# One decoder layer on one core: inputs laid out by the host, a new emission order, and a new last expert group

## The chip, the cores and the metric

The kernel runs on one core of a Trainium2 chip. TensorE (PE; its weight loads are PEld), VectorE (DVE), ScalarE (ACT) and GpSimd (POOL) each run their own queue in order; SyncE (SP) issues the DMAs. The metric is the device time of one execution in microseconds. The kernel before takes 398.06 us, the median of three runs from 396.9 to 398.94.

## The reference, cut to what matters

One layer for 256 tokens of width 1024 in float32: RMSNorm, one input projection (3592 columns) that feeds eight attention heads and four gated-DeltaNet heads, an output projection, a residual add; then RMSNorm and a mixture of 32 experts in four routing groups, of which each token uses two; a residual add and a last RMSNorm.

```
h = rmsnorm(x, attn_norm)
proj = einsum('bsd,de->bse', h, w_in)           # mq mk mv | gqkv gz ga gb
y_a = moba_attention(mq, mk, mv)
gqkv = silu(causal_depthwise_conv(gqkv, conv_w))
y_b = rmsnorm(gated_delta_rule(l2norm(gq), l2norm(gk), gv, log_decay, beta), gdn_norm) * silu(gz)
x = x + einsum('bse,ed->bsd', concat([y_a, y_b]), w_out)
h = rmsnorm(x, ffn_norm)
y = sum over experts e:  combine[t, e] * (silu(h @ w_gate[e]) * (h @ w_up[e])) @ w_down[e]
return rmsnorm(x + y, final_norm)
```

## The kernel before, in words

**Two halves.** The first half is everything up to the router. Its work is cut into some 300 named steps (generators that issue a few instructions each), and the long string `ORDER` says in which order the steps go out; each engine runs its own instructions in that order. The second half takes the experts four at a time: `NG` = 8 groups (not the routing groups). Every expert has three weight slabs of 1 MB (gate, up, down), so 96 MB go through SBUF. `load_expert` (L492) issues the next slab as soon as a buffer of 2048 columns is free; there are 25 such buffers, most of which serve the first half before, and become free there one by one. All loads go through SP's one queue, in order.

**The first half.** The input projection is done as three products of split numbers: weights are split into a high part (ACT cast, L561) and a low part (a subtraction, L563, on DVE or POOL as the string `LOW` says), and x likewise (`X.h`, L461 and L463: `hH`, `hL`). A piece `P0` to `P55` (L585, for one of the groups L594) is the twelve products of one block of 128 input channels with 512 output columns; pieces of one output group add up in two of the eight PSUM banks. x comes in by rows and is turned by sixteen PE transposes (`X.tr`, L414); `X.t` copies the turned x, `X.prm` turns the convolution weights; `X.sq`, `X.rs` and `X.bc` make the inverse root mean square, which the first readers of the banks need (`conv`, L614: a product, three taps L624, a last product L630 on DVE). The output projection (`W`, L1258) does the same split with `w_out`, whose columns stand interleaved by eight: the source of its casts and subtractions is read with a stride of eight.

**A group of experts.** DVE makes a selection matrix; PE gathers the tokens (L1439), multiplies with the gate and up slabs (L1455), DVE and ACT make the hidden activations (L1673 to L1685), PE multiplies with the down slabs (`down`, L1690), ACT copies the result to SBUF (L1702) and PE adds it into four banks by the transposed selection (`spread`, L1694).

**The last group.** Its up slabs come in three pieces each (`LASTU`), its down slabs in four column blocks `LAST` of 512, 256, 128 and 128, for all four experts before the next block. `keep` puts spare products (L1637) between the up products. While these end, DVE adds what the other groups summed to x (L1733). Per block: `down`, an ACT copy (L1768), `spread`, two DVE additions and two POOL products by the last gain (`finish`, L1744 and L1745), two ACT squares with row sums (`square`, L1750). `SPR` and `SQ` set how these interleave across blocks. Then DVE finds the inverse root of each half of the tokens (`rsqrt_steps`: a first guess from the number's bits and two refinements), three engines scale the rows, and two DMAs store them (L1790).

## Time and profile before

| | |
|---|---|
| median of the runs | 398.06 us |
| the profiled execution's own time | 400.69 us |
| its span, first to last instruction | 399.0 us |
| busy: PE, DVE, ACT, POOL | 344.1, 185.3, 111.1, 80.0 us |
| granted TensorE clock, mean | 0.966 of 2.4 GHz |
| DMA | 122.4 MB, 307 GB/s over the span |

The profile page divides the span into 40 slices: PE is over 80% busy in all but the last, DVE falls from nine tenths to two tenths after the first half, and the DMA engines are at nine tenths or more from slice 18 (180 us) to slice 37. Shares of the whole span mix these two halves, so each is read by itself below.

### The profile page before, as it was taken

What the parts mean: (1) busy time and instruction counts of PE and PEld (TensorE: products, weight loads), DVE (VectorE), ACT (ScalarE), POOL (GpSimd) and SP (SyncE); (2) the same over time, 40 slices, a digit from 0 to 9 for tenths busy, and PEclk for the clock granted to TensorE, in tenths of its full rate; (3) what the DMA queues carried; (4) which work ended last, traced back from release to release, by engine and by line L of the source; (5) the groups of instructions that cost most, each with busy time, mean ns of one, the idle gap of its engine ahead of it and who ended that gap; (6) DMA issues with size and microseconds to landing.
All of it is one profiled execution on the core that took longest, in us unless ns stands there. A gap on an engine that the chain in (4) does not pass through costs nothing. (4 is left out here: it accounts for less than half of the span.)

```text
span 399.0 us, 7995 instructions
## 1 busy us (share of the span) xinstructions
PE 344.1 (86%) x3323; PEld 249.9 (63%) x3323; DVE 185.3 (46%) x467; ACT 111.1 (28%) x240; POOL 80.0 (20%) x112
## 2 busy tenths in 40 slices
PE   3999989899989997988978969788797978979990
PEld 2999989897768886888742726245272532626540
DVE  3769899987726899336420121202012120123065
ACT  3765454634434456634001000010100001000032
POOL 7138334510842218430000000000000000000033
PEclk9999999999989999999899999899998999999996
DMA  8988556725303554989999999999999999999962
GB/s 287 266 294 330 218 163 244 251 86 212 107 0 107 168 207 175 415 291 373 414 387 421 413 422 418 408 421 418 409 424 421 406 419 421 409 423 397 343 178 106
DMA packets 35353, 122.40 MB, mean 307 GB/s; under 512 B 6082, under 2 KB 9203, under 8 KB 27635
## 3 DMA queue, kind: packets, MB, share of 16 engines
q1 hardware_dynamic: 35314, 121.87, 79.3%
q8 instruction: 27, 0.44, 0.4%
q14 instruction: 12, 0.09, 0.1%
HBM read 120.81 MB, written 1.05 MB: 305 GB/s over the span
## 5 line engine op out<-in xcount | busy, mean ns | idle before, releaser
L1442 DVE TENSOR_TENSOR B<-bank,late 128x512 f32<-128x512 f32 x16 | 11.1, 691 | 83.6 <-PE bank L1439 83.6
L1745 POOL TENSOR_TENSOR K<-K,B 128x128 f32<-128x128 f32 (+2 forms) x8 | 5.6, 734 | 209.9 <-DVE K L1744 209.9
L1694 PE MATMUL bank<-B,t1k 128*128 128x512 f32 (+2 forms) x72 | 32.1, 570 | 11.3 <-ACT B L1702 11.0
L1455 PE MATMUL bank<-B,B 128*32 128x256 f32 x240 | 40.1, 381 | 0.0
L1690 PE MATMUL bank<-B,t1k 128*32 128x512 f32 (+2 forms) x104 | 37.1, 696 | 1.0 <-DVE t1k L1685 1.0
L1702 ACT COPY B<-bank 128x512 f32<-128x512 f32 x14 | 8.2, 585 | 92.6 <-PE bank L1690 92.6
L1694 PEld LDWEIGHTS bank<-B,t1k 128*128 128x128 f32 x72 | 11.8, 189 | 35.1 <-ACT B L1702 26.7
L585 PE MATMUL bank<-hL,whl 128*128 128x256 f32 x192 | 31.3, 286 | 0.0
L585 PE MATMUL bank<-hH,whl 128*128 128x256 f32 x192 | 31.1, 286 | 0.0
L1455 PE MATMUL bank<-EX,B 128*32 128x256 f32 x368 | 28.6, 380 | 0.0
L1439 PEld LDWEIGHTS bank<-t1k,B 128*128 128x128 f32 x224 | 26.0, 192 | 2.9 <-issue 2.9
L1667 DVE COPY t1k<-bank 128x256 f32<-128x256 f32 x8 | 3.4, 424 | 51.9 <-PE bank L1665 51.9
L585 PEld LDWEIGHTS bank<-hL,whl 128*128 128x128 f32 x192 | 26.3, 191 | 0.7 <-issue 0.6
L585 PEld LDWEIGHTS bank<-hH,whl 128*128 128x128 f32 x192 | 26.3, 191 | 0.2
L1439 PE MATMUL bank<-t1k,B 128*128 128x128 f32 x224 | 26.1, 275 | 0.0
L1455 PE MATMUL bank<-K,B 128*32 128x256 f32 x144 | 26.0, 380 | 0.0
L1673 ACT ACTIVATE t1k<-bank 128x256 f32<-128x256 f32 x8 | 3.1, 383 | 75.4 <-PE bank L1455 66.5
L1690 PE MATMUL bank<-EX,t1k 128*32 128x512 f32 x64 | 22.2, 675 | 1.5 <-DVE t1k L1685 1.5
L561 ACT CAST whl<-RG 128x512 fp32r<-128x512 f32 x30 | 21.2, 727 | 7.3 <-PE bank L1258 3.5
L1455 PEld LDWEIGHTS bank<-B,B 128*32 128x32 f32 x240 | 19.0, 110 | 5.2
L1455 PEld LDWEIGHTS bank<-EX,B 128*32 128x32 f32 x368 | 15.2, 110 | 6.8
L1690 PE MATMUL bank<-whl,t1k 128*32 128x512 f32 (+2 forms) x56 | 18.0, 507 | 0.6 <-DVE t1k L1685 0.5
(381 smaller groups left out, 817.1 us busy)
## 6 DMA issues: line engine op xcount, KB each, us to landing
EX<-in_w_up_dram SPq DMA_DIRECT2D x16, 1024.0 KB, 15.0
B<-in_w_gate_dram SPq DMA_DIRECT2D x12, 1024.0 KB, 19.4
B<-in_w_down_dram SPq DMA_DIRECT2D x11, 1024.0 KB, 19.9
EX<-in_w_down_dram SPq DMA_DIRECT2D x8, 1024.0 KB, 20.0
EX<-in_w_gate_dram SPq DMA_DIRECT2D x7, 1024.0 KB, 9.6
B<-in_w_in_dram SPq DMA_DIRECT2D x5, 1024.0 KB, 5.5
RG<-in_w_in_dram SPq DMA_DIRECT2D x5, 1024.0 KB, 5.1
K<-in_w_gate_dram SPq DMA_DIRECT2D x5, 1024.0 KB, 19.4
```

Of the source, the lines that this page charges most:

```text
L561: S.copy(out=hv, in_=src)
L585: PE.matmul(o_, lhsT=a_[:, c4, j * P:(j + 1) * P], rhs=b_[:, c, :], start=(c == 0 and j % 2 == 0 and n == 0), stop=(c == KC - 1 and j % 2 ...
L1439: PE.matmul(ps[:, c4 * P:(c4 + 1) * P], lhsT=x2[tt][:, q * 4 + c4, :], rhs=Dsv[:, tt], start=(tt == 0), stop=(tt == 1))
L1442: V.tensor_tensor(out=xeT[:, q * 4:q * 4 + 4, :], in0=ps.rearrange("p (c s) -> p c s", c=4), in1=ffnT[:, q * 4:q * 4 + 4].unsqueeze(2).bro ...
L1455: PE.matmul(ps[r, 0:FF], lhsT=xeT[:, c, r], rhs=w[q][0][:, c, :], start=(c == 0), stop=(c == KC - 1), tile_position=(0, q * 32))
L1667: V.tensor_copy(out=DwT, in_=pt[:, 0:T])
L1673: S.activation(out=hid, in_=pgu[0][:, 0:FF], func=AF.Tanh, scale=0.5)
L1690: PE.matmul(ps[r, 0:w], lhsT=hv[:, ft, r], rhs=wd[q][0][:, ft, c0:c0 + w], start=(ft == 0), stop=(ft == 1), tile_position=(0, q * 32))
L1694: PE.matmul(ps[tt][:, 0:w], lhsT=DwT[:, tt * P:(tt + 1) * P], rhs=ye, start=(grp == 0 or last), stop=(grp >= NG - 2), skip_group_check=True)
L1702: S.copy(out=ye, in_=ps)
L1745: G.tensor_tensor(out=xf[:, tt, cs], in0=x3s[:, tt, cs], in1=fnB[:, cs], op=ALU.mult)
```

## The change

The host now hands over the inputs in the layout that SBUF wants (`_layout`): x turned (`xt`) beside x by rows, the small parameters in one array, `w_in` and `w_out` as whole tiles with 8 KB per partition (the interleaving of `w_out` undone), the down slabs with 8 KB per partition, and the last group's up and down slabs regrouped: an up slab is two blocks of input channels for all four experts, a down slab 256 output columns for all four. The PE transposes of x and of the convolution weights, and the copies behind them, go. `LAST` becomes 256, 256, 256, 128, 128; the interleaving by `SPR` and `SQ` goes. The last inverse root becomes one POOL instruction, a power of -0.5 on two columns. `ORDER` and `LOW` are new: 14 of 72 subtractions are on POOL, 22 before.

```
-LAST = ((0, 512), (512, 256), (768, 128), (896, 128))
-LASTU = ((0, 4), (4, 2), (6, 2))
+LAST = ((0, 256), (256, 256), (512, 256), (768, 128), (896, 128))
-SPR = (3, 2, 4, 4)
-CUT = (384, 512)
+CUT = 640
 ORDER = """
-C.b*8 X.d1 X.sq C.d*5 C.a*2 C.b*2 X.d3 X.d4 X.rs X.sq*2 X.rs X.tr0 X.tr1 X.d0 X.tr0*2 X.tr1*2 X.h0 X.rs*3 X.h0 ...
+C.b*5 X.h0 X.d0 X.h2 X.d1 X.h2 X.h1 C.a X.h0 X.h3 S0 S1 S0 X.d2 X.h1 C.b X.h3 C.b*2 R.k S1 P0 C.a P0*2 S2 P1 ...
-LOW = "VVVVGVGVVVVVVVVVVVVVVVGVGVVVVGVVVGGVVVGGVGVVGVGVGGGVVVGGVVVVVGVVGVGVGVVG"
+LOW = "VVVVVVVVVVVVVVVVVVVVVVVVVVVVGVVVVVVVVVGGVGVGGGVVVVVVVGGGVVVVVGVVVGGGVVVV"
...
+    nc.sync.dma_start(out=PAR[:, 0:64], in_=par[:, 0:64])
+    for k in range(4):
+        nc.sync.dma_start(out=xT[:, 2 * k:2 * k + 2, :], in_=xt[:, 2 * k:2 * k + 2, :])
+        if k == 1:
+            load_tile(0)
     load_tile(1)
+    nc.sync.dma_start(out=PAR[:, 64:NPAR], in_=par[:, 64:NPAR])
+    nc.sync.dma_start(out=view(B0, 0, 2, D), in_=x)
...
     def xh(c):
         def go():
-            src = st["xb"][c // 2][:, (c % 2) * T:(c % 2 + 1) * T]
+            src = xT[:, c, :]
...
-                src = view(raw[j], 0, 2, D)[:, w % 2, nh * 512:(nh + 1) * 512].rearrange("p (q c) -> p c q", c=KC)
+                src = view(raw[j], 0, 2, KC, P)[:, w % 2, nh * 4:(nh + 1) * 4, :]
...
+        if grp == NG - 1 and kind:
+            for k in range(2 if kind == 2 and q == EG - 1 else 1):
+                cs = slice(k * D, (k + 1) * D) if kind == 2 and q == EG - 1 else slice(0, 2 * D)
+                nc.sync.dma_start(out=t[:, cs], in_=(w_ul, w_dl)[kind - 1][q, :, cs])
...
+    pl = {}
+    for ci, (c0, w) in enumerate(LAST):
+        ps = bank()
+        for q in range(EG):
+            down(ps, q, c0, w)
+        ye = yes[:, c0:c0 + w]
+        S.copy(out=ye, in_=ps[:, 0:w])
+        banks.give(ps)
+        pl[ci] = [bank() for _ in range(2)]
+        spread(pl[ci], w, ye)
+        finish(ci)
+        for tt in range(2):
+            square(ci, tt)
...
+    G.tensor_tensor(out=rs3, in0=ms, in1=mhalf.broadcast_to([P, 2]), op=ALU.pow)
+    S.activation(out=xf[:, 1, 0:CUT], in_=xf[:, 1, 0:CUT], func=AF.Copy, scale=rs3[:, 1:2])
+    V.tensor_scalar(out=xf[:, 0, :], in0=xf[:, 0, :], scalar1=rs3[:, 0:1], scalar2=None, op0=ALU.mult)
+    V.tensor_scalar(out=xf[:, 1, CUT:], in0=xf[:, 1, CUT:], scalar1=rs3[:, 1:2], scalar2=None, op0=ALU.mult)
...
+def _layout(np, v):
+    win, wo = v["w_in"][0], v["w_out"][0]
+    tiles = np.stack([win[:, c0:c0 + 512].reshape(P, KC, 512)[:, hh * 4:hh * 4 + 4].reshape(P, 2048) for _, c0 in GROUPS for hh in range(2)])
+    wout = wo.reshape(4, 2, P, P, KC).transpose(0, 2, 1, 4, 3).reshape(4, P, 2048)
...
```

**SP, the first loads.** Before (x by rows, then the small parameters; `RG` and `B_86` take the first two weight tiles):

```order
L208 DMA B_79<-in_x_dram 128x1024 x2
L226 DMA K_59<-in_attn_norm_dram 128x8
L228 DMA K_59<-in_conv_w_dram 48x128
L229 DMA K_59<-in_gdn_norm_dram 1x128
L219 DMA RG_88<-in_w_in_dram 128x2x512 x2
L219 DMA B_86<-in_w_in_dram 128x4x512
L234 DMA K_59<-in_w_in_dram 128x8x8
```

Now (`xt` is the turned x, `par` the small parameters):

```order
L222 DMA K_59<-in_par_dram 128x64
L224 DMA B_80<-in_xt_dram 128x512 x2
L212 DMA RG_88<-in_w_in_dram 128x1024 x2
L224 DMA B_80<-in_xt_dram 128x512 x2
L212 DMA B_86<-in_w_in_dram 128x2048
L228 DMA K_59<-in_par_dram 128x256
L229 DMA B_79<-in_x_dram 128x2048
```

The turned x and the first weight tile lead; x by rows, which the root mean square is made from, has moved from the first place to the eleventh.

**PE, from its first instruction.** Before (L260 are spare products, L414 the transposes of x, L424 that of the convolution weights; the first piece, L585, comes behind the last row):

```order
L260 MATMUL bank_67<-K_58 128x256
L260 MATMUL bank_68<-K_58 128x256
L260 MATMUL bank_69<-K_58 128x256
L414 MATMUL bank_70<-late,B_79 128x128 x4
L260 MATMUL bank_74<-K_58 128x256
L414 MATMUL bank_71<-late,B_79 128x128 x2
L414 MATMUL bank_72<-late,B_79 128x128 x2
L414 MATMUL bank_71<-late,B_79 128x128 x2
L414 MATMUL bank_72<-late,B_79 128x128 x2
L414 MATMUL bank_73<-late,B_79 128x128 x2
L424 MATMUL bank_67<-late,K_59 128x49
L414 MATMUL bank_73<-late,B_79 128x128 x2
```

Now (L252 are the spare products, L531 the pieces):

```order
L252 MATMUL bank_67<-EX_94 128x256
L252 MATMUL bank_68<-EX_94 128x256
L252 MATMUL bank_69<-EX_94 128x256
L531 MATMUL bank_70<-hH,whl_99 128x256 x2
L531 MATMUL bank_71<-hH,whl_99 128x256 x2
L531 MATMUL bank_70<-hL,whl_99 128x256 x2
L531 MATMUL bank_71<-hL,whl_99 128x256 x2
```

The first piece now follows the spare products directly.

**ACT, the last group.** Before (L1768 copies a block's `down` result, L1750 squares a finished block, L1787 scales the output):

```order
L1768 COPY B_81<-bank_69 128x512
L1768 COPY B_81<-bank_67 128x256
L1750 ACTIVATE EX_93,late<-K_60 128x512
L1768 COPY B_81<-bank_71 128x128
L1750 ACTIVATE EX_93,late<-K_60 128x512
L1750 ACTIVATE EX_93,late<-K_60 128x256
L1768 COPY B_81<-bank_74 128x128
L1750 ACTIVATE EX_93,late<-K_60 128x256
L1750 ACTIVATE EX_93,late<-K_60 128x128 x4
L1787 ACTIVATE K_58<-K_58,late 128x384 x2
```

Now (L1710 copies, L1702 squares, L1724 scales):

```order
L1710 COPY B_81<-bank_67 128x256
L1702 ACTIVATE B_80,late<-K_60 128x256 x2
L1710 COPY B_81<-bank_68 128x256
L1702 ACTIVATE B_80,late<-K_60 128x256 x2
L1710 COPY B_81<-bank_73 128x256
L1702 ACTIVATE B_80,late<-K_60 128x256 x2
L1710 COPY B_81<-bank_72 128x128
L1702 ACTIVATE B_80,late<-K_60 128x128 x2
L1710 COPY B_81<-bank_71 128x128
L1702 ACTIVATE B_80,late<-K_60 128x128 x2
L1724 ACTIVATE K_58<-K_58,late 128x640
```

Before, a copy stood ahead of the squares of the block before it. Now both squares of a block stand ahead of the next block's copy.

## Rows read from the trace of the kernel before

**Rows 1.** Timeline, PE: start us, duration us, line, out<-in, shapes, count, idle before

```profile
13.94 0.83 PE L585 MATMUL bank<-hH,whl 128*128 128x256 f32 x4
...
30.18 0.64 PE L585 MATMUL bank<-hH,mixA 128*128 128x256 f32 x4
30.66 0.64 PE L585 MATMUL bank<-hH,whl 128*128 128x256 f32 x4
```

**Rows 2.** Timeline of the first 6 us: the load of x, its first reader

```profile
0.80 0.87 SPq L208 DMA_DIRECT2D B<-in_x_dram  x2
...
4.24 1.06 ACT L401 ACTIVATE B<-B 128x1024 f32<-128x1024 f32 x1 [2.16 <-DMA B<-in_x_dram]
```

**Rows 3.** Windows: length, PE, PEld, DVE, ACT, POOL busy, PEclk, DMA share, GB/s

```profile
30.00:80.00 50.00, 47.15 (x433) 45.83 (x433) 46.59 (x92) 26.71 (x57) 24.51 (x36) 1.00 0.67 241
```

**Rows 4.** Groups by form, DVE, 10 to 185 us: count | busy us, mean ns | idle

```profile
L563 DVE TENSOR_TENSOR mixB<-B,whl 128x512 fp32r<-128x512 f32 x12 | 12.6, 1058 | 0.9 <-ACT whl L561 0.9
...
L563 DVE TENSOR_TENSOR whl<-RG,whl 128x512 fp32r<-128x512 f32 x4 | 6.1, 1546 | 7.7 <-ACT whl L561 7.7
...
L563 DVE TENSOR_TENSOR mixA<-EX,whl 128x512 fp32r<-128x512 f32 x4 | 2.8, 689 | 2.5 <-ACT whl L561 2.5
```

**Rows 5.** The same for POOL

```profile
L563 POOL TENSOR_TENSOR mixB<-B,whl 128x512 fp32r<-128x512 f32 x8 | 10.9, 1366 | 17.8 <-ACT whl L561 13.8 <-DVE t1k L624 4.0
...
L445 POOL TENSOR_SCALAR K<-K 128x2 f32<-128x2 f32 x1 | 0.4, 420 | 0.0
```

**Rows 6.** Timeline, PE: first rows of the output projection and of what follows it

```profile
153.53 0.50 PE L1258 MATMUL bank<-mixA,B 128*128 128x256 f32 x2
...
181.14 3.66 PE L1287 MATMUL bank<-B,B 128*128 128x36 f32 x32
```

**Rows 7.** Timeline, PE: two gathers, the first work of two groups of experts

```profile
313.77 3.73 PE L1439 MATMUL bank<-t1k,B 128*128 128x128 f32 x32
...
338.41 3.73 PE L1439 MATMUL bank<-t1k,B 128*128 128x128 f32 x32
```

**Rows 8.** Windows in the second half

```profile
325.00:330.00 5.00, 2.92 (x14) 0.87 (x18) 2.23 (x6) 0.00 (x0) 0.00 (x0) 0.74 1.00 413
345.00:365.00 20.00, 16.24 (x145) 7.56 (x138) 3.79 (x8) 1.55 (x3) 0.00 (x0) 1.00 1.02 414
365.00:385.00 20.00, 18.63 (x209) 11.07 (x208) 8.37 (x13) 0.97 (x2) 0.01 (x1) 1.00 0.99 336
```

**Rows 9.** Timeline of all engines, 380 to 395 us

```profile
380.19 3.98 DVE L1733 TENSOR_TENSOR K<-bank,B 128x512 f32<-128x512 f32 x4
...
380.33 0.62 PE L1690 MATMUL bank<-whl,t1k 128*32 128x512 f32 x1
...
384.97 0.11 PEld L1690 LDWEIGHTS bank<-mixB,t1k 128*32 128x32 f32 x1 [0.76 <-DMA mixB<-in_w_down_dram]
...
386.42 0.37 ACT L1768 COPY B<-bank 128x256 f32<-128x256 f32 x1 [3.46 <-PE bank L1690]
...
386.85 1.13 PE L1694 MATMUL bank<-B,t1k 128*128 128x256 f32 x4 [0.36 <-ACT B L1768]
...
387.58 0.85 DVE L1744 TENSOR_TENSOR K<-K,bank 128x256 f32<-128x256 f32 x2 [1.81 <-PE bank L1694]
...
388.08 0.41 ACT L1750 ACTIVATE EX<-K 128x256 f32<-128x256 f32 x1
...
389.03 0.99 DVE L1744 TENSOR_TENSOR K<-K,bank 128x128 f32<-128x128 f32 x4 [0.59 <-PE bank L1694]
...
390.24 0.29 ACT L1750 ACTIVATE EX<-K 128x128 f32<-128x128 f32 x1
...
390.87 0.30 DVE L1779 SCALAR_TENSOR_TENSOR late<-late 128x1 f32<-128x1 f32 x1
...
392.66 0.48 DVE L1789 TENSOR_SCALAR K<-K,late 128x512 f32<-128x512 f32 x1
...
393.43 1.50 SPq L1790 DMA_DIRECT2D out_dram<-K  x2
```

More of the change, by code (lines that the diff above doesn't have):

```diff
@@ L200, in hybrid_layer_kernel @@
     wrS = view(B4, 1760, KC, 36)
-    x0 = x[0]
     out0 = out[0]
-    win = w_in[0].rearrange("(p c) n -> p c n", c=KC)
-    for tt in range(2):
-        nc.sync.dma_start(out=xnat[tt], in_=x0[tt * P:(tt + 1) * P, :])
     raw = {}
@@ L214, in load_tile @@
         if i < 2 * len(GROUPS):
-            c0, hh = GROUPS[i // 2][1], i % 2
-            v = view(t, 0, 4, 512)
-            for k in range(2 if i == 0 else 1):
-                ks = slice(2 * k, 2 * k + 2) if i == 0 else slice(0, 4)
-                nc.sync.dma_start(out=v[:, ks, :], in_=win[:, hh * 4 + ks.start:hh * 4 + ks.stop, c0:c0 + 512])
+            n = 2 if i == 0 else 1
+            for k in range(n):
+                ks = slice(k * 2048 // n, (k + 1) * 2048 // n)
+                nc.sync.dma_start(out=t[:, ks], in_=w_in[i, :, ks])
@@ L405, in _ @@
         S.activation(out=junk[:, 1, 512:D], in_=xnat[1][:, 512:D], func=AF.Square, accum_out=ssq[:, 2:3])
-    def xtr(tt):
-        def go():
-            if tt == 0:
-                st["xb"] = [bank() for _ in range(4)]
-            xv = xnat[tt].rearrange("t (p c) -> t c p", c=KC)
-            for c in range(KC):
-                o_ = (c % 2) * T + tt * P
-                PE.transpose(out=st["xb"][c // 2][:, o_:o_ + P], in_=xv[:, c, :], identity=ident)
-                if c % 2 and c < KC - 1:
-                    yield
-        return go
-    steps["X.tr0"], steps["X.tr1"] = xtr(0), xtr(1)
-    @step("X.prm")
-    def _():
-        ps = bank()
-        PE.transpose(out=ps[:, 0:49], in_=prm, identity=ident[0:49, 0:49])
-        yield
-        S.copy(out=prT, in_=ps[:, 0:49])
-        yield
-        S.copy(out=gn_col, in_=ps[:, 48:49])
-        banks.give(ps)
     @step("X.rs")
@@ L464, in xh @@
         return go
-    def xcopy(b):
-        def go():
-            S.copy(out=xT[:, 2 * b:2 * b + 2, :], in_=st["xb"][b].rearrange("p (c t) -> p c t", c=2))
-            banks.give(st["xb"][b])
-        return go
     for c in range(KC):
         steps[f"X.h{c}"] = xh(c)
-    for b in range(4):
-        steps[f"X.t{b}"] = xcopy(b)
     for i in range(NEX):
@@ L1649, in hybrid_layer_kernel @@
             if grp or ki:
-                for i, _ in enumerate(products(pgu[ki], wx)):
+                for i, _ in enumerate(products(pgu[ki], wx, last and ki)):
                     if last and ki:
@@ L1750, in square @@
         S.activation(out=sq3[:, tt, c0:c0 + w], in_=x3s[:, tt, c0:c0 + w], func=AF.Square, accum_out=ss3[:, tt, ci:ci + 1])
-    pl, yl = {}, {}
-    SQ = {1: ((0, 0),), 2: ((0, 1), (1, 0)), 3: ((1, 1), (2, 0), (2, 1)), 4: ((3, 0), (3, 1))}
-    for ci in range(NL + 1):
-        if ci < NL:
-            c0, w = LAST[ci]
-            ps = bank()
-            for q in range(EG):
-                if ci and q == SPR[ci]:
-                    pl[ci - 1] = [bank() for _ in range(2)]
-                    spread(pl[ci - 1], *yl[ci - 1])
-                down(ps, q, c0, w)
-        if ci and ci - 1 not in pl:
-            pl[ci - 1] = [bank() for _ in range(2)]
-            spread(pl[ci - 1], *yl[ci - 1])
-        if ci < NL:
-            yl[ci] = (w, yes[:, c0:c0 + w])
-            S.copy(out=yl[ci][1], in_=ps[:, 0:w])
-            banks.give(ps)
-        if ci:
-            finish(ci - 1)
-        for a in SQ.get(ci, ()):
-            square(*a)
+    pl = {}
```

178 lines of the change are left out of this document (80 added, 98 removed).

## The prediction, made before the changed kernel was run

> **What bounds the kernel now.** I read the page's slices first: PE is busy nearly throughout, and the DMA engines are full from 180 us on, so one of the two sets the second half, and the page alone does not say which. Three views decide it.
>
> The timeline of PE comes first. The first useful product starts at 13.94 us; from there pieces follow each other at 0.48 us per four products [rows 1], that is 0.12 us for one, and PE is busy for 47.15 of the 50 us between 30 and 80 us [rows 3]. So in the first half PE is the bound, with DVE close behind: 46.59 of the same 50 us. What starts PE earlier moves the router earlier, if DVE keeps up.
>
> Then the second half. Its DMA rate is flat at 414 GB/s until 365 us [rows 8], which looks like a DMA bound. But two groups of experts begin 24.64 us apart on PE (338.41 - 313.77, [rows 7]), and twelve slabs of 1.05 MB take 30.4 us at 414 GB/s. PE runs faster than its data; it can, because two whole groups are loaded when it starts, and this lead shrinks by some 5.8 us per group. It is just used up at the end: the only wait for a slab that I find in the last group is 0.76 us, at 384.97 [rows 9]. So the end is set by PE's own chain, and the DMA stands right behind it.
>
> Last the tail. From the first `down` of the last group at 380.33 [rows 9] to the span's end at 399.0 are 18.7 us: four additions on DVE until 384.17, four blocks, the inverse root, the scaling, and the stores from 393.43 on.
>
> **The change part by part**, against the profiled execution's 400.69 us (span 399.0, and 1.7 around it), which lies 2.6 above the median of 398.06.
>
> *The start.* PE waits in the first 14 us for x, sixteen transposes and the casts behind them. Now P0 needs the parameters, the first quarter of the turned x and the first half tile. The first half megabyte of x lands 3.4 us after its issue at 0.80 [rows 2]. In the new queue half a megabyte of turned x leads, then the half tile, another 1.3 us at 414 GB/s, so it is there at about 5.6 to 6.1; a cast and the gap before the product make it 6.6 to 7.2. That is 13.94 - 6.9 = 7.0 us earlier, bounds 6 and 7.5. Behind it one megabyte per 2.5 us arrives, and four pieces (one tile) take PE 5.8, so later tiles are in time. I find PE's work after P0 unchanged.
>
> *LOW and the order.* 14 of 72 subtractions are on POOL, 22 before; of the 56 of the input projection 10 instead of 17. Seven more on DVE at 0.69 (rows without disturbance, [rows 4]) are 4.8 us in a stretch in which DVE is idle for 3.4 of 50. Against it: beside POOL's subtractions (1.37 each, [rows 5]) DVE's own take 1.06 instead of 0.69; twelve of them lose 4.4 us, and seventeen moved to ten give back 7/17 of it, 1.8. Net +3.0 on DVE. The earlier tiles let DVE do some eight subtractions before the first convolution, 5.5 us of lead, so DVE is ahead by less than PE, and PE will wait for it. I charge +1.5. Bounds: +5 if all of it lands on PE; -3 if the new order removes waits that the old one has.
>
> The Trainium skill ("SBUF — State Buffer", "SBUF: two separate sides") says that DVE and GpSimd share a port pair, and that a DVE instruction with two SBUF inputs and a GpSimd one lock each other out for a whole instruction. The 1.06 beside 0.69 agrees. By that rule each of the seven moved could give back up to POOL's 1.37, and the term would be nearer the lower bound.
>
> *The output projection.* 192 products from 153.53 to 181.14 take 27.6 us [rows 6]; at 0.12 each they would take 23.0. The rest is waiting for splits read with stride eight: 1.55 per subtraction on DVE against 0.69 [rows 4]. Without the stride I take -3.0 of the 4.6, bounds 0 and -5 (a little of the stage before as well). The router's steps stay in their order: 0.
>
> *The groups.* The same instructions, and PE's own chain: 0. Larger rows of the down slabs move no faster where 414 GB/s is reached now. But the granted clock drops to 1.2 GHz after the gap before `down` in some groups, as at 325 us with a mean of 0.74 [rows 8], which cost 1.3 us of PE there. These stretches fall differently when the work is moved: +-3.4, no direction.
>
> *The tail.* Time is counted from the first `down`. DVE is in its four additions until 384.17 (380.19 + 3.98), which is 3.9 us later, whatever PE has done, so the first block's own additions start there; its second square ends 1.3 later (0.43 for an addition, then two squares of 0.41), and only then may ACT take the next copy: 5.2. From copy to copy a block of 256 takes 0.43 (386.42 to 386.85) + 0.73 (to the addition at 387.58) + 0.43 + 0.07 + 2 x 0.41 = 2.5 [rows 9]. The copies are at 5.2, 7.7, 10.2; a block of 128, with additions of 0.25 and squares of 0.29, I estimate at 1.7: 11.9, and its last square starts at 13.3. From a last square to the next DVE step it is 0.63 (390.24 to 390.87): 13.9; two such steps 0.3; the power: no row shows it, the nearest is POOL's two-column operation of 0.42 [rows 5]; bounds 0.2 and 2.0, which is what the chain of DVE takes that it replaces (390.87 to 392.66, 1.8). So 14.7. DVE then scales 1024 and 384 columns, from 0.48 per 512, 1.4 us; the store's issue is 0.45, and what follows the last issue is 399.0 - 394.93 = 4.1. Sum 20.7, against 18.7: +2.0, bounds -1.5 and +4. The root itself saves 1.4; the squares ahead of the copies cost more.
>
> Sum: -7.0 + 1.5 - 3.0 + 0 + 2.0 = -6.5 us, so 394.2 for an execution like the profiled one and, 2.6 lower, 391.6 for the median.
>
> **The rivals.** *The DMA is the bound after all.* From 365 to 385 us the rate is 336 instead of 414 [rows 8]: 1.56 MB, or 3.8 us, lost on small pieces and on the row of issues. If the slabs were what the last group waits for, the start (-7.0) and these 3.8 would both count, and the tail would be paced by slabs 2.5 us apart, so that the root's 1.4 is saved too: -12.2, a median of 385.9. For it: 414 GB/s without a break, and the 0.76 us. Against it: 24.64 against 30.4 us per group, and no other wait. Chance 0.18. The skill's rule ("DMA: Bandwidth & Descriptors", "Specifications") that 512 B per transfer is enough for line rate would take the 3.8 away: the smallest pieces here have 512 B rows. The 336 GB/s speak against it, as far as waiting issues are not the cause.
>
> *DVE takes it back (slower).* x by rows, from 0.80 in the queue, now stands behind some 3 MB, at about 14 us instead of 4.2. Without its root no bank of the projection can be read. PE has eight banks, six for three output groups, so it can run 24 pieces, 34.6 us, ahead. If the first convolution starts later than some 31 us, PE stops there: the start's 7 us are lost, the net +3.0 on DVE stay, the tail's +2.0 comes to it, and the output projection gives -3.0: +2.0 or more, a median near 400 to 402. Against it: by my count DVE reaches the convolution at about 28 to 30. Chance 0.13.
>
> *It does little.* PE starts early but waits as much at other places, as an order of 300 steps can easily do: only the output projection's 3.0 against the tail's 2.0, and a median of 397. Chance 0.14.
>
> **How the numbers follow.** The forecast has 0.55, with 388 to 396 as its own range. The range of 384.5 to 399.5 takes in the first rival's most, the third, and leaves out the second. Within 0.5% (2.0 us, about what a measurement of this kernel can tell from no change) is 396.1 to 400.0. Faster: the forecast, the first rival and a quarter of the third, 0.77. Same: most of the third and a little of the second, 0.12. Slower: 0.11.
>
> **What would show it.** Right: the first piece at 6.6 to 7.2 us; the router's first product near 174 instead of 181.14; gathers still 24 to 25 us apart; the output projection in 24 to 25 us; copies 2.5 us apart in the last group, and 20 us or more from the first `down` to the end. Wrong: PE waits for the additions or subtractions of DVE between 40 and 80 us (second rival); waits of the products for slabs in the last two groups (first rival); a power above 1 us; a `down` that starts later than DVE's four additions end.

## The result, and the profile after

The changed kernel takes 395.6 us (median of 10 runs, 391.89 to 397.25), the kernel before 399.41 on the same chip (10 runs, 396.9 to 402.0): a ratio of 0.9896, 95% interval 0.9858 to 0.9935. The forecast was 6.5 us less; it is about 4. In the ratios here and below, runs more than 1.5% above the fastest of their kernel are left out; the medians hold all runs. The profiled executions have spans of 393.6 and 399.0 us, 5.4 apart. Where these come from, by the marks of PE's chain (us; product n is the one with n products of the projection before it; a stage's change is the difference of the two differences):

| mark | before | after | after - before | stage alone |
|---|---|---|---|---|
| first projection product | 13.94 | 8.90 | -5.0 | -5.0 |
| product 240 of the projection | 45.06 | 42.75 | -2.3 | +2.7 |
| first product of the output projection | 153.53 | 144.76 | -8.8 | -6.5 |
| router's first product | 181.14 | 170.67 | -10.5 | -1.7 |
| first gather | 191.40 | 180.68 | -10.7 | -0.2 |
| last group's gather | 363.65 | 351.21 | -12.4 | -1.7 |
| copy of the last hidden layer, turned | 379.85 | 372.24 | -7.6 | +4.8 |
| end of the span | 399.0 | 393.6 | -5.4 | +2.2 |

So the front half gained more than forecast (10.5 instead of 8.5 at the router), from other terms than forecast, and the last group gave 4.8 back at a place that the forecast had at zero.

The start, in the timeline of the changed kernel (start us, duration us; in brackets the idle time before and what ended it). It answers to [rows 1] and [rows 2]:

```profile
1.26 2.93 PE L252 MATMUL bank<-EX 128*128 128x256 f32 x6 [1.26 <-DVE EX L241]
...
5.34 1.28 ACT L427 ACT_TABLE_LOAD   x1 [5.34 <-DMA B<-in_xt_dram]
...
6.64 1.70 ACT L427 ACTIVATE hH<-B,K 128x256 fp32r<-128x256 f32 x4
...
8.25 1.64 ACT L507 CAST whl<-RG 128x512 fp32r<-128x512 f32 x3
...
8.90 1.22 PE L531 MATMUL bank<-hH,whl 128*128 128x256 f32 x4 [4.72 <-ACT whl L507]
...
9.93 1.05 PE L531 MATMUL bank<-hL,whl 128*128 128x256 f32 x4
...
15.33 0.64 PE L531 MATMUL bank<-hH,mixA 128*128 128x256 f32 x4
```

The first quarter of the turned x lands at 5.27 and the first half of a weight tile at 7.41, where the forecast had both by 5.6 to 6.1. ACT's table load (1.28 us) waits behind the turned x: it goes out with ACT's first activation. Then four activations stand ahead of the first cast, which starts at 8.25. And PE, idle for 4.72 us after its spare products, starts at half speed: 0.85 from four products to the next four until 14 us, then 0.48. The windows of the same stretch show the granted clock (columns as in [rows 3]; PEclk is the third from the right): 0.50 is 1.2 GHz, 1.00 is 2.4 GHz.

```profile
8.00:10.00 2.00, 1.10 (x5) 1.10 (x6) 1.58 (x5) 1.89 (x4) 0.00 (x0) 0.50 1.01 277
...
12.00:14.00 2.00, 2.00 (x12) 2.00 (x11) 1.47 (x3) 0.25 (x1) 0.00 (x0) 0.50 1.03 423
...
16.00:18.00 2.00, 2.00 (x20) 1.84 (x23) 2.00 (x4) 1.76 (x4) 1.94 (x4) 1.00 1.01 426
```

The last group begins with a wait that has no row before. PE's timeline:

```profile
350.31 1.06 PE L1671 MATMUL bank<-late 128*128 128x128 f32 x8
351.21 0.50 PE L1385 MATMUL bank<-t1k,B 128*128 128x128 f32 x3
354.64 5.13 PE L1385 MATMUL bank<-t1k,B 128*128 128x128 f32 x29 [2.94 <-issue]
```

The gather is cut after three products, 2.94 us pass in which PE waits for nothing that the trace shows ("issue"), and it goes on at a granted clock of 0.83 in the mean of 350 to 360 us. The gathers of [rows 7] took 3.73 us in one piece. Just ahead of it (L1664) stands the branch for tokens over an expert's capacity.

The tail, all engines, answering to [rows 9]:

```profile
372.58 3.92 DVE L1685 TENSOR_TENSOR K<-bank,B 128x512 f32<-128x512 f32 x4
...
372.71 1.09 PE L1642 MATMUL bank<-RG,t1k 128*32 128x256 f32 x16
373.90 0.37 ACT L1710 COPY B<-bank 128x256 f32<-128x256 f32 x1 [10.09 <-PE bank L1642]
...
374.33 1.13 PE L1646 MATMUL bank<-B,t1k 128*128 128x256 f32 x4 [0.52 <-ACT B L1710]
...
375.39 1.09 PE L1642 MATMUL bank<-whl,t1k 128*32 128x256 f32 x16
376.42 0.74 DVE L1696 TENSOR_TENSOR K<-K,bank 128x256 f32<-128x256 f32 x2
376.86 0.42 ACT L1702 ACTIVATE B<-K 128x256 f32<-128x256 f32 x1 [2.59 <-DVE K L1696]
...
377.68 0.35 ACT L1710 COPY B<-bank 128x256 f32<-128x256 f32 x1
378.08 1.13 PE L1646 MATMUL bank<-B,t1k 128*128 128x256 f32 x4 [1.60 <-ACT B L1710]
...
380.38 0.37 ACT L1710 COPY B<-bank 128x256 f32<-128x256 f32 x1 [0.17 <-PE bank L1642]
...
386.81 0.73 POOL L1723 TENSOR_TENSOR late<-late 128x2 f32<-128x2 f32 x1 [0.17 <-DVE late L1722]
387.57 0.83 ACT L1724 ACTIVATE K<-K,late 128x640 f32<-128x640 f32 x1 [1.14 <-POOL late L1723]
```

From the first `down` to the end 20.9 us, forecast 20.7. The second copy comes right behind the first block's squares, which waited for DVE, as the forecast has it. The third ends a wait for PE (L1642), not for the squares: the first sign that the reason given is not the whole one.

The slabs of the last group: 420 GB/s from 360 to 365 us; the first that `down` needs lands at 363.31, 9.4 us ahead of it, and the last at 370.75. In the group before, it is otherwise. There the `down` products of four experts go out side by side when their slabs are there (at 345.50 and 345.54 in the second half of that step). In the first half the fourth expert's comes late, first in the kernel before, then in the changed one:

```profile
352.15 1.50 PE L1690 MATMUL bank<-EX,t1k 128*32 128x512 f32 x9 [0.52 <-DVE t1k L1685]
353.40 0.62 PE L1690 MATMUL bank<-B,t1k 128*32 128x512 f32 x1
```

```profile
339.85 1.51 PE L1642 MATMUL bank<-EX,t1k 128*32 128x512 f32 x9 [0.52 <-DVE t1k L1631]
340.96 0.62 PE L1642 MATMUL bank<-B,t1k 128*32 128x512 f32 x1
```

Its slab (`B`) lands at 353.36 and 340.92: the product starts 0.04 us later, and does so in the traces of all twelve experiments too. The last group's gather follows 10.29 us after this landing in both kernels, and 9.95 to 11.15 us after it in all fourteen traces. No idle time of PE shows this here, as the other three experts' products keep the engine busy.

### The profile page after: what moved, and what is told of

Its sections match the earlier page's. It is cut to its first block, busy times and chain, and to the rows that moved or that the text cites. A ratio compares the mean times of both kernels' runs of the same rounds, so it can differ in the third digit from the quotient of the medians.

```text
span 393.6 us, 7941 instructions
## 1 busy us (share of the span) xinstructions
PE 340.6 (87%) x3326; PEld 249.0 (63%) x3326; DVE 179.2 (46%) x460; ACT 101.1 (26%) x238; POOL 65.5 (17%) x106
## 5 line engine op out<-in xcount | busy, mean ns | idle before, releaser
L1646 PE MATMUL bank<-B,t1k 128*128 128x512 f32 (+2 forms) x76 | 34.4, 576 | 14.7 <-ACT B L1654 11.0
L1697 POOL TENSOR_TENSOR K<-K,whl 128x256 f32<-128x256 f32 (+1 forms) x10 | 6.0, 619 | 218.5 <-DVE K L1696 218.5
L1401 PE MATMUL bank<-EX,B 128*32 128x256 f32 x416 | 39.6, 380 | 0.0
L1401 PE MATMUL bank<-B,B 128*32 128x256 f32 x240 | 38.0, 380 | 0.0
L531 PE MATMUL bank<-hH,whl 128*128 128x256 f32 x192 | 32.7, 295 | 4.8 <-ACT whl L507 4.7
L1642 PE MATMUL bank<-B,t1k 128*32 128x512 f32 (+1 forms) x104 | 33.7, 670 | 1.0 <-DVE t1k L1631 1.0
L531 PE MATMUL bank<-hL,whl 128*128 128x256 f32 x192 | 32.1, 292 | 0.0
L531 PEld LDWEIGHTS bank<-hH,whl 128*128 128x128 f32 x192 | 27.6, 199 | 6.3 <-ACT whl L507 5.7
L531 PEld LDWEIGHTS bank<-hL,whl 128*128 128x128 f32 x192 | 27.1, 197 | 0.9 <-DVE mixB L509 0.4
L1401 PEld LDWEIGHTS bank<-EX,B 128*32 128x32 f32 x416 | 20.4, 110 | 6.5
L1401 PE MATMUL bank<-K,B 128*32 128x256 f32 x144 | 22.9, 380 | 0.0
L507 ACT CAST whl<-RG 128x512 fp32r<-128x512 f32 x30 | 17.7, 613 | 10.5 <-DMA RG<-in_w_in_dram 4.4
L509 DVE TENSOR_TENSOR mixA<-RG,whl 128x512 fp32r<-128x512 f32 x22 | 16.4, 762 | 3.6 <-ACT whl L507 3.6
L531 PE MATMUL bank<-hH,mixA 128*128 128x256 f32 x96 | 16.6, 298 | 0.6 <-DVE mixA L509 0.6
```

Of the source, the lines that this page charges most:

```text
L507: S.copy(out=hv, in_=src)
L509: (G if LOW[i] == "G" else V).tensor_tensor(out=lv, in0=src, in1=hv.bitcast(FP32), op=ALU.subtract)
L531: PE.matmul(o_, lhsT=a_[:, c4, j * P:(j + 1) * P], rhs=b_[:, c, :], start=(c == 0 and j % 2 == 0 and n == 0), stop=(c == KC - 1 and j % 2 ...
L1401: PE.matmul(ps[r, 0:FF], lhsT=xeT[:, c, r], rhs=w[c // 2][0][:, c % 2, q, :] if mixed else w[q][0][:, c, :], start=(c == 0), stop=(c == KC ...
L1642: PE.matmul(ps[r, 0:w], lhsT=hv[:, ft, r], rhs=rhs, start=(ft == 0), stop=(ft == 1), tile_position=(0, q * 32))
L1646: PE.matmul(ps[tt][:, 0:w], lhsT=DwT[:, tt * P:(tt + 1) * P], rhs=ye, start=(grp == 0 or last), stop=(grp >= NG - 2), skip_group_check=True)
```

## The experiments

All are the changed kernel with one edit (e2 and e6 have two, e11 three), and are compared with the kernel before on the same chip, where its median is 399.09 (e1 to e4), 398.29 (e5 to e8) or 399.75 us (e9 to e12). The times of several fall into two clusters, some 5 us apart; e3 tells why. A trace is one execution: a mark that moves is told from chance by the other traces in which that stretch is unedited.

| run | median us (runs) | ratio to before, 95% |
|---|---|---|
| changed kernel | 395.6 (10) | 0.9896 (0.9858 to 0.9935) |
| e1_table | 392.62 (4) | 0.9817 (0.9741 to 0.9894) |
| e2_warm | 395.12 (4) | 0.9891 (0.9796 to 0.9987) |
| e3_nobranch | 388.96 (4) | 0.9737 (0.9697 to 0.9777) |
| e4_stride | 400.98 (10) | 1.0045 (1.0012 to 1.0078) |
| e5_squares | 394.26 (9) | 0.9866 (0.9812 to 0.9920) |
| e6_adds | 394.45 (10) | 0.9833 (0.9772 to 0.9893) |
| e7_root | 395.55 (10) | 0.9906 (0.9862 to 0.9950) |
| e8_low | 400.9 (10) | 1.0077 (1.0034 to 1.0120) |
| e9_order | 393.39 (4) | 0.9831 (0.9767 to 0.9895) |
| e10_late_branch | 391.1 (4) | 0.9785 (0.9723 to 0.9847) |
| e11_all | 386.1 (6) | 0.9655 (0.9611 to 0.9699) |
| e12_pieces | 397.04 (10) | 0.9941 (0.9906 to 0.9977) |

**e1: the table load first.**

```
     V.memset(warm, 0.0)
+    S.activation(out=LATE(1), in_=warm[:, 0:1], func=AF.Copy, scale=1.0)
```

> The changed kernel with one tiny copy on ACT at the start that waits for nothing but the cleared spare tile, so that ACT's table load (1.28 us, at 5.34 behind the wait for the turned x in the changed kernel) comes at about 1 us. Theory (the start gave less because the table load stands in the chain to P0): P0 at about 7.6 instead of 8.90 us, all later work 1.3 us earlier, 0.4% off the changed kernel's time. Rival (the clock decides: P0's products run at 1.2 GHz until about 17 us whatever their start): P0 at 7.6, but product 48 is earlier by less than 0.7 us. Rival (the turned x lands later than the load ends anyway): P0 stays within 0.3 us of 8.90.

P0 starts at 7.81 instead of 8.90, product 48 at 16.01 instead of 17.25, the output projection at 143.53 instead of 144.76: 1.1 to 1.2 us. But the changed kernel's trace is at the late end of a spread. In the nine traces whose instructions up to there are the changed kernel's (its own, e3 to e7, e9, e10 and e12), P0 starts at 8.20 to 9.23, product 48 at 15.49 to 17.25 and the output projection at 143.13 to 145.00. So P0 gains 0.4 to 1.4 us, and in e11, which has the same edit, it is at 8.00; a gain behind it is not shown (product 48 in e11 is at 16.07). The rival of the clock stays open: the full clock is back at 13.2 us in e1, and at 11.5 to 14.6 in the nine. The four runs of e1 are 390.03, 390.14, 395.1 and 395.23.

**e2: PE kept busy until P0.** As e1, and:

```
-        steps[f"X.d{i}"] = lambda: dummies(1)
+        steps[f"X.d{i}"] = lambda i=i: dummies(3 if i < 3 else 1)
```

> As e1_table, and nine spare products instead of three before P0, so that PE is busy from 1.3 to about 7 us. Theory (the idle 4.72 us before P0 let the granted clock fall, and the first pieces then took 0.85 us per four products instead of 0.48 until about 17 us): P0 at 7.2 to 7.8, the granted clock at 0.95 or more between 8 and 20 us, product 48 at 13.5 to 14.5 instead of 17.25. Whether that is kept: if PE is the bound behind it, product 240 comes 2.5 to 4 us before 43.23 and the kernel takes 390 to 392.5 on the changed kernel's 395.6; rival (DVE or the arrival of the tiles paces the pieces from 15 us on): product 240 within 1.5 us of 43.23, time within 1.5 us of the changed kernel.

P0 starts at 8.22, later than expected, but the first pieces run at full speed (0.48 from four products to the next), and product 48 comes at 14.21, 3.0 us ahead of the changed kernel and 1.3 ahead of the earliest of the nine traces. Product 96 comes at 23.27 (23.40 to 25.05 in the nine), product 240 at 40.96 (41.09 to 42.75; the 43.23 of the expectation is four products further on), and the output projection at 143.95, amid the spread. Windows of e2:

```profile
10.00:20.00 10.00, 9.75 (x84) 8.45 (x82) 7.06 (x21) 7.25 (x16) 4.97 (x10) 1.00 1.02 422
20.00:30.00 10.00, 9.62 (x77) 9.51 (x78) 9.26 (x30) 4.84 (x12) 0.92 (x3) 1.00 0.79 311
```

PE now has idle time at 20 to 30 us (0.4 us), where it had none; its one named wait there is for DVE (0.6 us), and DVE is at 9.26 of 10. At product 240 the gain of 1.8 lies between the theory's 2.5 and the rival's 1.5, at the output projection it is the rival's: what the clock gives PE in the first 14 us is taken back behind it. That it is DVE that takes it is what these rows suggest; no run here shows it alone.

**e3: the branch left out.**

```
-            cmax = nc.values_load(cmi, min_val=0, max_val=T)
-            with tc.If(cmax > CAP):
-                overflow(fs)
```

> The changed kernel without the branch for tokens over an expert's capacity ahead of the last group (leaves out that path, which these inputs do not take). Theory (the 2.94 us in which PE waits for nothing shown, amid the last group's gather, come of the branch in PE's instruction stream): no such wait in the last group, the gather's products at 0.11 instead of 0.15 us, from the gather's first product to the copy of the turned hidden layer 16 to 17.5 us instead of 20.86, 1% off the time. Rival (it is a wait for instructions that falls anywhere, or chance of one execution): a wait of 2 to 3 us without a releaser is found at another place, or none in either, and the time stays within 0.5%.

The gather takes 3.74 us in one piece, from it to the copy of the turned hidden layer are 16.20 us instead of 21.03, and the runs lie in one cluster, 387.88 to 390.04: 6.6 us below the changed kernel's median. PE's timeline of e3:

```profile
350.20 1.04 PE L1668 MATMUL bank<-late 128*128 128x128 f32 x8
351.07 3.74 PE L1385 MATMUL bank<-t1k,B 128*128 128x128 f32 x32
```

The two clusters of the others are executions with and without this wait, as far as the traces tell: two of those with the branch ahead of the gather have no wait, those of e2 (392.65) and e5 (388.95; its runs are 388.95 to 389.71, and 393.4 to 395.95), both in the low cluster; eight have it. The trace of the kernel before has the branch and no wait. Its runs on all chips, 395.21 to 402.82, show no second cluster, but whether some of them have the wait is not known. What PE waits for can be read in the DMA queues. This is the changed kernel from 352 to 353 us (queue, kind: packets, MB, share of 16 engines):

```profile
q1 hardware_dynamic: 60, 0.42, 100.3%
q8 instruction: 1, 0.02, 6.9%
```

One packet of instructions, 16 KB, starts there, at 352.3, among slab packets that fill all engines. PE goes on at 354.64, 2.3 us after. In e1 the packet starts at 351.5 and PE goes on at 354.02, in e9 at 354.2 and 356.68, in e12 at 349.3 and 351.84: 2.3 to 2.5 us in all eight traces with the wait. In all eight the packet starts 1.0 to 2.1 us after PE's first product behind the branch (350.31 in the changed kernel), and exactly eleven products, the eight spare ones and three of the gather, go out before PE stands. In e2, in e5 and in the kernel before, without the wait, a packet starts 3.1 to 6.9 us ahead of that product. In e10 and e11, with the branch elsewhere, one starts at 352.95 and 352.87, amid the gather, and PE does not stop. This, and that the wait goes with the branch, is why I read it as a wait for instructions; no row names it so.

**e4: the stride back in the output weights.**

```
-                src = view(raw[j], 0, 2, KC, P)[:, w % 2, nh * 4:(nh + 1) * 4, :]
+                src = view(raw[j], 0, 2, P, 2, 4)[:, nh, :, w % 2, :].rearrange("p q c -> p c q")
```

> The changed kernel with the output weight laid out on the host so that its splits read with a stride of eight elements, as the kernel before did. Theory (the stride is what the output projection lost): subtractions of the output weight at 1.5 us on DVE instead of about 0.7, output projection from first product to the router's first 27 to 29 us instead of 25.9, time up 0.5 to 1%. Rival (the splits are done ahead, and the stage is bound elsewhere, by the softmax and the products of the stage before): subtractions at 1.5 but the stage within 0.7 us of 25.9.

From the first product (144.67) to the router's (175.83) 31.2 us instead of 25.9; the runs go up by 1.4%. DVE's groups by form from 140 to 178 us, first in e4, then in the changed kernel, answering to [rows 4] (count | busy us, mean ns | idle us):

```profile
L509 DVE TENSOR_TENSOR B<-K,B 128x512 fp32r<-128x512 f32 x4 | 5.2, 1310 | 5.0 <-ACT B L507 5.0
...
L509 DVE TENSOR_TENSOR whl<-RG,whl 128x512 fp32r<-128x512 f32 x2 | 3.7, 1842 | 1.8 <-ACT whl L507 1.8
```

```profile
L509 DVE TENSOR_TENSOR B<-K,B 128x512 fp32r<-128x512 f32 x4 | 2.8, 722 | 4.1 <-ACT B L507 4.1
...
L509 DVE TENSOR_TENSOR whl<-RG,whl 128x512 fp32r<-128x512 f32 x2 | 2.5, 1234 | 1.9 <-ACT whl L507 1.9
```

In this order the stride costs 5.3 us; in the kernel before, the stage had 27.6 with it [rows 6], only 1.7 above the 25.9. Why it lost less there no run shows. And without the stride the subtractions are not all at 0.69.

**e5: squares behind the next copy.**

```
         for tt in range(2):
-            square(ci, tt)
+            if ci:
+                square(ci - 1, tt)
+    for tt in range(2):
+        square(NL - 1, tt)
```

> The changed kernel with each block's two squares in the last group issued on ACT behind the next block's copy, and the last block's at the end. Theory (the tail grew because ACT's squares, which wait for DVE's additions, stand ahead of the next copy): copies at most 2.0 us apart after the second instead of 2.7 and 2.5, from the first down product to the end 18 to 19 us instead of 20.9. Rival (DVE's four additions until 376.5 and the block's own additions behind them set the pace, not ACT): copies closer, but the last square within 0.7 us of the changed kernel's, tail 20.2 to 20.9.

The tail is 19.6 us (367.33 to 386.9), 1.3 less (it is 20.5 to 20.9 in the seven traces with this tail unedited), but the copies are still 2.7 apart: neither theory nor rival. ACT and PE in e5's timeline:

```profile
371.19 0.37 ACT L1710 COPY B<-bank 128x256 f32<-128x256 f32 x1 [2.30 <-PE bank L1642]
...
371.61 1.13 PE L1646 MATMUL bank<-B,t1k 128*128 128x256 f32 x4 [0.52 <-ACT B L1710]
...
372.67 1.09 PE L1642 MATMUL bank<-B,t1k 128*32 128x256 f32 x16
373.92 0.37 ACT L1710 COPY B<-bank 128x256 f32<-128x256 f32 x1 [1.53 <-PE bank L1642]
```

ACT now waits for PE at every copy, and PE for ACT at every `spread`: copy, 0.42 to the spread, 1.06 for it, 1.25 for the next `down` and the hand-over make the 2.73. PE's order has the next `down` behind the spread that waits for the copy. The order with `SPR` in the kernel before had not.

**e6: the four additions earlier.** As e5, and the loop of the four additions (L1685) moved up:

```
             for q in range(2):
                 run(gather(grp, q))
+        if last:
+            x3s = view(fs[2], 0, 2, D)
+            for nh in range(2):
...
```

> As e5_squares, and DVE's four additions of the residual (3.92 us, at 372.58 in the changed kernel) moved to right behind the last group's gather, where DVE waits for PE. Theory (both stand on the path of the tail): the first block's own addition starts less than 1.2 us after the first copy instead of 2.5, from the first down product to the end 16 to 17.5 us, 1% off the changed kernel's time. Rival (the additions, moved ahead, delay what DVE does for the products of the last group): the time from the last gather to the copy of the turned hidden layer grows by 1 us or more and takes part of it back.

The first block's own addition starts 1.16 us after its copy, as the theory has it, and yet the tail stays at 19.6 (374.31 to 393.9): with the squares moved, the additions are not on the path. (The additions alone were not moved.) From the gather to the copy it is 22.1 us instead of 21.0, but all of this lies in the gather with its wait (9.68 instead of 8.56), behind which both take 12.46: the rival has no part in it. No gain beyond e5: the medians are 394.45 and 394.26.

**e7: the roots on DVE again.**

```
-    G.tensor_tensor(out=rs3, in0=ms, in1=mhalf.broadcast_to([P, 2]), op=ALU.pow)
+    run(*[rsqrt_steps(rs3[:, tt:tt + 1], ms[:, tt:tt + 1], 1, LATE) for tt in range(2)])
```

> The changed kernel with the inverse roots by DVE's chain of steps, as in the kernel before, instead of one power on GpSimd. Theory (prediction: the power saves 1.4 us): from the last square to the first scaling 1.0 to 1.6 us more than in the changed kernel. Rival (two hand-overs to GpSimd and the additions still queued there eat the gain): within 0.5 us of it.

From the reading of the last square's sum to the first scaling 1.98 us (386.61 to 388.59) instead of 1.32 (386.25 to 387.57): the power saves 0.7 us, half of what was forecast; the runs can't tell it.

**e8: LOW of the kernel before.**

```
-LOW = "VVVVVVVVVVVVVVVVVVVVVVVVVVVVGVVVVVVVVVGGVGVGGGVVVVVVVGGGVVVVVGVVVGGGVVVV"
+LOW = "VVVVGVGVVVVVVVVVVVVVVVGVGVVVVGVVVGGVVVGGVGVVGVGVGGGVVVGGVVVVVGVVGVGVGVVG"
```

> The changed kernel with the kernel before's assignment of the splits' subtractions (22 on GpSimd instead of 14), in the changed order. Theory (prediction: seven more subtractions on DVE cost PE some 1.5 us between the start and the router): the router's first product 1 to 3 us before 170.7. Rival (DVE and GpSimd hold each other up, and GpSimd's subtraction takes twice as long, so a split on GpSimd comes later to PE): the router's first product 0.5 to 4 us after 170.7, DVE's mean per subtraction higher.

The rival holds, beyond its range: the output projection begins at 149.22 instead of 144.76, the router at 175.28, 4.6 us late. Product 240 is early in this trace (41.35), so from there to the output projection it is 107.9 us instead of 102.0, 5.9 more. PE's longest wait in e8, and DVE's group by form from 9 to 145 us:

```profile
62.95 0.88 PE L531 MATMUL bank<-hH,mixA 128*128 128x256 f32 x4 [3.73 <-DVE mixA L509]
```

```profile
L509 DVE TENSOR_TENSOR mixB<-B,whl 128x512 fp32r<-128x512 f32 x12 | 11.0, 922 | 2.0 <-ACT whl L507 1.9
```

That form took 1058 ns in the kernel before [rows 4], and takes this in the changed kernel:

```profile
L509 DVE TENSOR_TENSOR mixB<-B,whl 128x512 fp32r<-128x512 f32 x15 | 11.3, 767 | 2.0 <-ACT whl L507 2.0
```

POOL's own take 1.3 to 1.5 in both. The order was written with the new `LOW`, so the run tells what `LOW` is worth in this order, not by itself.

**e9: PE's order in the tail.** `down` of the next block ahead of `spread` of this one, squares two copies later:

```
+    for ci in range(NL + 2):
+        if ci < NL:
+            for q in range(EG):
+                down(ps, q, c0, w)
+            S.copy(out=yes[:, c0:c0 + w], in_=ps[:, 0:w])
...
+        if 0 < ci <= NL:
...
+            spread(pl[ci - 1], w, yes[:, c0:c0 + w])
+            finish(ci - 1)
+        if ci > 1:
+            for tt in range(2):
+                square(ci - 2, tt)
```

> The changed kernel with PE's order in the last group changed: the down products of the next block stand ahead of the spreading of this one, and each block's squares stand two copies later on ACT. Theory (after e5 and e6: the 2.7 us from copy to copy are PE's own round: down, ACT's copy, spread, and only then the next down): copies about 2.0 to 2.1 us apart for blocks of 256, from the first down product to the span's end 17 to 18 us instead of 20.9 (19.6 with the squares alone moved). Rival (DVE's residual additions until 3.9 us after the copy of the turned hidden layer, or banks of PSUM not yet free, hold the third block): copies still 2.5 or more apart, 19 us or more.

Copies at 375.94, 376.81, 378.95, 380.56 and 382.22, 0.9 to 2.1 apart; from the first `down` to the end 17.0 us (374.76 to 391.8) instead of 20.9, with the additions where they were. The theory holds. PE in e9:

```profile
374.76 1.09 PE L1642 MATMUL bank<-RG,t1k 128*32 128x256 f32 x16
...
375.64 1.09 PE L1642 MATMUL bank<-whl,t1k 128*32 128x256 f32 x16
...
376.66 1.13 PE L1646 MATMUL bank<-B,t1k 128*128 128x256 f32 x4
...
377.72 1.09 PE L1642 MATMUL bank<-B,t1k 128*32 128x256 f32 x16
...
378.74 1.13 PE L1646 MATMUL bank<-B,t1k 128*128 128x256 f32 x4
```

No wait is left between them.

**e10: the branch later**, between the last group's hidden activations and their transposes.

```
             cmax = nc.values_load(cmi, min_val=0, max_val=T)
-            with tc.If(cmax > CAP):
-                overflow(fs)
-            fnB = view(fs[0], 0, D)
+            fnB = view(fs[4], 0, D)
...
         banks.give(*pgu)
+        if last:
+            with tc.If(cmax > CAP):
+                overflow(fs)
```

> The changed kernel with the branch for tokens over capacity moved from ahead of the last group's gather to behind its products, where PE waits 1.3 us for DVE anyway and the slabs have all landed. Theory (the wait in the gather ends when an instruction packet of 16 KB lands, which in most executions comes late because of the branch and behind the slabs): no wait in the gather, times in one cluster as in e3_nobranch, 388 to 391, with up to 2 us left for the branch in the tail. Rival (the packet is late whenever the transfers are full, branch or not): the wait stays in most executions and the median at 395.

One cluster, 390.05 to 392.84, the gather in one piece (3.74), 16.25 us to the copy of the hidden layer. The branch costs nothing visible there: PE waits 1.4 us ahead of the transposes, as it did for DVE (1.3).

**e11: e1, e9 and e10 together.**

> The early table load of e1_table, the order of e9_order and the late branch of e10_late_branch together in the changed kernel. Theory (the three are at different places of PE's chain, so they add): 1.3 + 3.3 + 5 = 9 to 10 us below the changed kernel's median, 385 to 388, ratio to the kernel before 0.965 to 0.975. Rival (the front moves earlier and the slabs of the last groups become the bound, as the single wait of 0.6 us for a slab in e2_warm suggests): waits for slabs of 1 us or more in the last two groups and 388 or more.

386.1 us, 385.93 to 387.11, a ratio of 0.9655: the fastest kernel here, 9.5 us below the changed one. By the marks, the front is 1.1 earlier at the router, but the last gather starts at 351.37, no earlier than in the changed kernel (351.21). From there to the copy 16.26, and from the first `down` 17.1 to the end. So the tail and the branch add; of the start nothing is seen, and the 1.1 at the router are no more than the spread (169.66 in e9 and 169.40 in e10, without the early table load). PE's waits from 300 us on, in e11 (what waited, line <- for what: us in total, times, longest):

```profile
PE bank L1629 <- DVE t1k L1622: 3.3, 2, 1.6
...
PE bank L1646 <- DMA B<-in_w_down_dram: 0.6, 1, 0.6
```

The second row is the seventh group's `down`. That step takes 9.8 us in e11 from its first product to the end of its last, 7.6 in the changed kernel; its last slab lands at 341.42, 0.5 later than in the changed kernel (340.92), and the gather follows 9.95 us after. So up to the last gather the slabs take back what PE is early. Waits of 0.5 to 0.6 us for the same slab are in e2, e5, e6, e9 and e10 too, so it is not e11's start that brings them.

**e12: smaller pieces for the last group.**

```
-            for k in range(2 if kind == 2 and q == EG - 1 else 1):
-                cs = slice(k * D, (k + 1) * D) if kind == 2 and q == EG - 1 else slice(0, 2 * D)
+            for k in range(8):
+                cs = slice(k * 256, (k + 1) * 256)
```

> The changed kernel with the last group's eight slabs of up and down loaded in eight pieces of 128 KB each (rows of 1 KB instead of 8 KB). It tests the first rival of the prediction, that the last group's transfers were what larger rows could speed up. Theory (PE sets the end, the slabs land with some 8 us to spare): the transfers end 1 to 5 us later than 364, no wait of PE for a slab over 1 us, time within 1 us of the changed kernel's. Rival (the transfers are the bound or close): waits of PE for slabs of 2 us or more, time up by as much. Aside: if the instruction packet waits behind slab packets, smaller ones should make the wait in the gather rarer or shorter.

Windows of e12:

```profile
350.00:355.00 5.00, 3.16 (x19) 3.17 (x20) 1.71 (x3) 0.00 (x0) 0.00 (x0) 0.78 0.69 198
...
370.00:375.00 5.00, 4.20 (x40) 2.42 (x40) 4.47 (x7) 0.37 (x1) 0.00 (x0) 1.00 0.87 222
375.00:380.00 5.00, 4.21 (x26) 1.78 (x22) 1.29 (x4) 2.17 (x10) 2.82 (x4) 1.00 0.87 281
```

The rate falls from 420 to 198 to 281 GB/s, the transfers last beyond 380, and two `down` rows stretch from 1.09 to 1.95 and 2.42 us: 2.2 us late. The median is 1.4 us above the changed kernel's, which the two intervals do not tell apart. By the trace the rival holds for these pieces. SP issues eight of 128 KB in 3.74 us, which is 280 GB/s, so the issues set the rate at least in part. The wait in the gather is still there (2.13 us); smaller packets did not take it away.

## Why the prediction was right or wrong, by its steps

**What bounds.** Right for the last group, not for the way there. e3, e9 and e10 shorten PE's chain behind the last gather, and the time follows. But the last gather is timed by a slab of the seventh group, in the kernel before as in the changed one. PE's other products were ready 1.2 and 1.1 us before this slab (352.15 and 339.85), in e9 4.9 us, and the gather still comes 10.29 us after the landing. "The only wait for a slab that I find in the last group is 0.76 us" looked one group too late. The lead of the slabs that the prediction works out (5.8 us lost per group) is used up there. Nor is PE over 80% busy in all slices but the last of the page before: it is below that in the first and in eight others, seven of them from slice 20 on.

**The start: the step that failed most.** "It is there at about 5.6 to 6.1; a cast and the gap before the product make it 6.6 to 7.2": the half tile lands at 7.41, and at 7.12 in e1, where the cast follows at 7.14 and P0 at 7.81. So most of what is missing at P0 is the landing; the table load and four activations on ACT held the cast another 0.8 us in the changed kernel. And "I find PE's work after P0 unchanged" left out the clock: from P0 to product 48 it is 8.35 us, at a granted clock of 0.50 until 14.6, against 5.94 in the kernel before and 5.99 in e2. So product 240 gains 2.3 us of the 7.0 forecast (4.0 in the earliest of the nine traces). With table and clock repaired (e2) it gains 4.1, but of the 1.8 in which e2 is ahead of the changed kernel there 0.8 are left at the output projection.

**LOW and order: the wrong sign.** Charged at +1.5 within -3 to +5; from product 240 to the output projection PE gained 6.5. e8 gives back 5.9 of it. The step counted +3.0 us on DVE; it is +1.6 (46 subtractions of the projection take 33.6 us, where 39 took 32.0). The commonest form, `mixA<-RG`, stayed at 0.76 in the mean (0.75 before); `mixB<-B` fell to 0.77 from 1.06: 15 of them take 11.3 us, where 12 took 12.6 [rows 4]. What failed is "PE will wait for it": PE's idle time in this stretch is 2.2 us, 6.6 in the kernel before, and 6.4 in e8, more than half of it the one wait shown there. The Trainium skill's rule ("SBUF — State Buffer", "SBUF: two separate sides"), that DVE with two SBUF inputs and a GpSimd instruction that reads SBUF lock each other out, spoke for the lower bound. The runs agree in direction: 922 ns with 22 on POOL, 767 with 14. What the lock alone is worth, beside POOL's longer subtraction (1.3 to 1.5 us), no run here separates.

**The output projection.** -1.7 instead of -3.0. The stride itself is worth 5.3 us in this order (e4), more than the forecast's upper bound of 5; the kernel before was only 1.7 longer with it, and the subtractions into `whl` still take 1.23.

**The groups.** 0 within 3.4: -1.9 from the router to the last gather, of which the first group has 1.5 (27.5 us between the first two gathers before, 26.0 after); then +4.8 in the last group. "The same instructions" was right and not enough: the fetch of these instructions is a transfer too, and it came late, as I read the packets; that the branch ahead of the gather brings the wait is shown (e3, e10). Without this term the runs are at 388 to 390 (e3), below the 391.6 forecast.

**The tail.** 20.9 instead of 20.7, +2.2 instead of +2.0: the size right, the reason right in part. The second copy does stand behind the squares and these behind DVE, 5.0 us after the first `down` (5.2 forecast). But freeing it gains only 1.3 (e5), and moving the additions as well gains nothing more (e6): then PE's order sets the pace, and with it changed the gain is 3.9 in all (e9). The root saves 0.7 (e7) instead of 1.4.

**The sum.** -5.4 by the spans, -3.8 by the medians, forecast -6.5. That it came so near is in good part luck: the start gave 4.7 us less and the wait in the gather took 4.8 that were not in the sum, and LOW and order gave 8.0 more.

**The rivals.** *The DMA as the bound:* not for the last group, whose first slab for `down` lands 9.4 us ahead of it, and whose copies no slab paces; but a slab does set the last gather, so up to there its condition held. Its -12.2 did not come. e12 shows what the new slabs were for: with small pieces the earlier PE would have run into the transfers. The Trainium skill's rule that 512 B are enough for line rate ("DMA: Bandwidth & Descriptors", "Specifications") is not confirmed by 198 to 281 GB/s with 1 KB rows, nor refuted, as the issues limit e12 as well. *DVE takes it back:* no wait of PE between 40 and 80 us above 0.6; but what e2 gains and loses again looks like that mechanism, for what the warm clock adds. *It does little:* closest in the total (397), for none of its reasons.

**Open.** Why the instruction packet comes late in most executions of the changed kernel and not in the trace of the kernel before. The transfers are full in both, and the packets of slab data larger now; e12 speaks against their size as the only cause. And why the seventh group's last slab lands at 338.9 to 342.7 us in traces whose router starts within 2 us.

## What to carry to other kernels

An early start is worth what stands behind it lets through: look at the landing of the first weights, the clock, the second engine's lead, and the next place where a product starts just as its load lands, before counting it. Such a place need not show as idle time of the engine: compare the landing with the start of the product that reads it. Where PE's order has a product wait for a copy of the product just before it, put the next independent one between them. A branch in the middle of saturated transfers can leave PE without instructions; put it where PE waits anyway.
